# Turning the FFN's gated products with transposing transfers in place of TensorE transposes

## The chip, the cores and the metric

The kernel runs on one core of a Trainium2 chip. The core has five engines that work beside each other: TensorE (PE, matrix products; its weight loads are listed as PEld), VectorE (DVE), ScalarE (ACT), GpSimd (POOL) and SyncE (SP), which here issues transfers. Each engine takes its instructions in the order of its own queue, and they wait for each other on semaphores. Transfers between the device's memory and the on-chip memory SBUF run on 16 DMA engines. TensorE writes to PSUM, eight banks of 128 x 512 float32.

The metric is the device time of one execution in microseconds (us), as the median of several runs. Lower is better.

## The reference

The reference is an encoder trunk of two layers over 256 tokens of width 1024. Each layer has two mixing branches (gated linear attention and grouped-query attention), an output projection, a gated feed-forward block (FFN) and an embedding that is added per layer, each with RMS norms around it. What the change touches is the FFN, whose hidden width is 2816:

```python
gate, up = jnp.split(rms_norm(h, g_ffn_pre) @ w_ffn_in, 2, axis=-1)
h = h + rms_norm((jax.nn.silu(gate) * up) @ w_ffn_out, g_ffn_post)
```

## The kernel before

**Products in split form.** Every operand of a matmul is kept as two parts of TensorE's reduced float32 format: a high part, which is the value rounded, and a low part, which is what the rounding left. A product is three passes: high by high, high by low, low by high. `split` (line 133) makes the parts: ACT casts the value to the high part, DVE subtracts it from the value for the low part. Weights are loaded in units of 128 x 2048 float32 (1 MB) into `raw` tiles or lent buffers, split in two pieces of 128 x 1024, and held in four pairs of buffers `wh` and `wl`. `Stream` runs ahead: when a unit has been used, `ws.done()` lets the next unit be split (as long as fewer than four are held) and the next load be issued (line 296) on SP's queue.

**What is turned, and why.** A matmul contracts over the partition dimension. A result has tokens in partitions and columns of the hidden layer along the row; the next product needs the hidden columns in partitions. So the gated products, `silu(gate) * up`, are turned in blocks of 128 x 128. `transpose_in` (lines 440 to 449) does it: TensorE transposes against an identity matrix into one PSUM bank (`aux`), then ACT and DVE split the bank into the tile that holds the turned product in high and low parts (`Split.put`, line 133 again). These tiles belong to `hid`, a `Split`: group k // 4 holds four blocks of 128 hidden columns for both halves of the tokens.

**The FFN's order.** The 2816 hidden columns are 11 blocks of 256. Blocks 0 and 1 are computed first, one token half (128 tokens, `hf`) after the other (L1566 and the product behind it). Blocks 4, 5 and 10 (`PLAIN`) are computed by `block`, both halves together (L1584). The other six are three pairs, blocks 2 and 3, 6 and 7, 8 and 9 (`PAIRS`), computed by `seven`, a form of Strassen's method: seven products in place of eight, with sums of weights made on DVE and four sums of activations (`sums`) made once; `gated` (L1608) is called for one half at step 6 and for the other at step 7. The three strings of `FFN` set the order: `u` is half a plain block, a digit a step of a pair, `o` the product of one block with `w_ffn_out`, in the order of `OUT` = 0, 1, 2, 3, 4, 5, 10, 6, and then, in the stage `ffnout`, 7, 8, 9. `out_step` makes those output products (its matmuls are listed at L105, as those of the FFN's first product are at L121). It calls `hid.need`, which makes sure that the turned blocks it reads have been put into the program.

**Tasks and ticks.** A turn is a `Task`: a generator that yields how many ticks to wait. `tick()` is called twice in every 12 matmuls or so; at each tick the tasks whose count is over go on. Blocks 0 and 1 wait 4 ticks (`WAIT_FFN`), plain blocks 6 (`WAIT_BLOCK`, L1592 is their transpose), pairs 9 (`WAIT_PAIR`), the last pair 3 and 4 (`WAIT_LAST`).

**The planner.** The kernel's text gives the order in which instructions are written down, and from it their priority. A planner then orders each engine's queue: it simulates the engines and takes, among the instructions that it holds ready, the one of the highest priority. `tc.high_priority(AHEAD)` raises the priority of what stands under it; `tc.issue_after` fixes an order. The planner also puts in the waits and gives out the buffers: ten `mid` tiles (128 x 1024 float32), five `t512` tiles, nine `big` tiles, eight PSUM banks. An instruction that needs a buffer waits until one is free.

Of the kernel before, what the change touches and what calls it, by code (L numbers as in the profile page):

```python
# [10 lines left out]
F32 = mybir.dt.float32  # L11
F32R = mybir.dt.float32r
BF16 = mybir.dt.bfloat16
AF = mybir.ActivationFunctionType
ALU = mybir.AluOpType
AX = mybir.AxisListType

P = 128
T = 256
# [4 lines left out]

AHEAD, EMPTY, EMPTY_FIRST = 400, 100, 1600

WAIT, WAIT_FIRST, WAIT_FFN, WAIT_BLOCK = 6, 4, 4, 6

WAIT_NEXT, WAIT_IN, WAIT_H = (7, 9), ((6, 9), (6, 6)), ((3, 5), (3, 5))
WAIT_MIX = 3, 6  # L30
# [11 lines left out]
PLAIN, PAIRS = (4, 5, 10), (2, 6, 8)  # L42
OUT = (0, 1, 2, 3, 4, 5, 10, 6, 7, 8, 9)

WAIT_PAIR, WAIT_LAST = 9, (3, 4)


GATES = "uuu1u2m34m5m67m"
# [11 lines left out]
def trunk_kernel(ctx: ExitStack, tc: tile.TileContext, a: dict, out: bass.AP):  # L60
# [7 lines left out]
    nc = tc.nc  # L68
# [11 lines left out]
    part = ["start"]  # L80

    def nm(s):
        uid[0] += 1
        return f"{s}_{part[0]}_{uid[0]}"
# [4 lines left out]
    def mid(dt=F32):  # L89
        return b4p.tile([P, 1024], dt, tag="mid", name=nm("mid"))  # L90

    def acc():
        return accp.tile([P, 512], F32, tag="acc", name=nm("acc"))

    def aux():
        return accp.tile([P, 512], F32, tag="acc", name=nm("aux"))

    def t512():
        return smp.tile([P, 512], F32, tag="t512", name=nm("t512"), bufs=5)
# [25 lines left out]
    def vmul(out, in0, in1):  # L125
        nc.vector.tensor_tensor(out=out, in0=in0, in1=in1, op=ALU.mult)
# [4 lines left out]
    def split(hi, lo, src):  # L131

        return nc.scalar.copy(hi, src), nc.vector.tensor_tensor(out=lo, in0=src, in1=hi.bitcast(F32), op=ALU.subtract)  # L133


    h = cp.tile([P, 2, D], F32, tag="h", name="h")
    line = {}

    def on(e, f, *args, **kw):

        with tc.issue_after(line[e].ins) if e in line else nullcontext():
            line[e] = f(*args, **kw)

    seed = cp.tile([P, P], BF16, tag="seed", name="seed")
    on("pool", nc.gpsimd.memset, seed, 1.0)
    keep = cp.tile([P, 512], BF16, tag="keep", name="keep")
    on("dve", nc.vector.memset, keep, 1.0)
# [13 lines left out]
    ident = cp.tile([P, P], F32, tag="ident", name="ident")  # L161
# [279 lines left out]
    def transpose_in(sp, src, k, n, hf, plain=None):  # L441

        ps = aux()
        for i in range(n):
            nc.tensor.transpose(ps[:, i * P : (i + 1) * P], src[:, i * P : (i + 1) * P], ident)
        with tc.high_priority(AHEAD):
            sp.put(ps[:, : n * P], k, n, hf * P, P)
        if plain is not None:
            nc.scalar.copy(plain, ps[:, : n * P])

    last_pow = [None]

# [13 lines left out]
    def split_by(hi, lo, src, r):  # L466

        nc.scalar.activation(hi, src, AF.Copy, bias=0.0, scale=r)
        nc.vector.scalar_tensor_tensor(
# [5 lines left out]
    def row_rstd(parts, behind=None):  # L475
# [5 lines left out]
        for j, src in enumerate(parts):  # L481
# [9 lines left out]
            else:  # L491
                with tc.issue_after(behind.ins) if j and behind is not None else nullcontext():
                    last_square[0] = nc.scalar.activation(
                        junk[:, :n], src, AF.Square, scale=1.0 / 32.0, accum_out=ss[:, j : j + 1]
                    )
# [19 lines left out]
    def halves(t):  # L515
        return [t[:, j * 512 : (j + 1) * 512] for j in range(2)]
# [24 lines left out]
    def pre_gain(g, hf, sp, wait, to):  # L541
# [8 lines left out]
        with tc.high_priority(EMPTY):  # L550
            ss = small(2, "ss")
            for j in range(2):
                last_square[0] = nc.scalar.activation(t512(), x[j], AF.Square, scale=1.0 / 32.0, accum_out=ss[:, j : j + 1])
            r = rs[hf]
# [32 lines left out]
    def last_norm(parts, g, hf):  # L587

        with tc.high_priority(AHEAD):
            yt, junk, ss, r, c = mid(), mid(), small(3, "ss"), small(1, "rstd"), 0  # L590
            cuts = []
            for src in parts:
                cuts.append(slice(c, c + src.shape[-1]))
                c += src.shape[-1]
            nc.scalar.activation(junk[:, cuts[0]], parts[0], AF.Square, scale=1.0 / 32.0, accum_out=ss[:, 0:1])
            nc.vector.scalar_tensor_tensor(
# [16 lines left out]
            for j, c in enumerate(cuts):  # L613
                x = h[:, hf, c]
                if j == 1:
                    nc.scalar.activation(yt[j], yt[j], AF.Copy, bias=0.0, scale=r)
                    nc.gpsimd.tensor_tensor(out=x, in0=yt[j], in1=x, op=ALU.add)
# [4 lines left out]
    def amode(o, sp, hf, k0, w, first, last, c0=0, fresh=False):  # L622

        wh, wl = (t[:, :2048].rearrange("p (k c) -> p k c", c=512)[:, :, c0 : c0 + o.shape[-1]] for t in w)
        sp.need(hf, k0)
        parts = [(sp.tok(k0 + k, hf), (wh[:, k, :], wl[:, k, :])) for k in range(4)]
        passes(o, parts, first, last, fresh, tick if o.shape[-1] == 512 else None)
        tick()
# [100 lines left out]
    def project_t(sp):  # L729

        o = [acc(), acc()]
        for kh in range(2):
            wmode(o, sp, kh * 4, ws.take(), kh == 0, kh == 1)
            ws.done()
        return o

    def project(sp):

        o = [acc(), acc()]
        for kh in range(2):  # L740
            w = ws.take()
            for hf in range(2):
                amode(o[hf], sp, hf, kh * 4, w, kh == 0, kh == 1)
            ws.done()
        return o
# [97 lines left out]
    def square(hf, j):  # L843
        on("act", nc.scalar.activation, t512(), hv(hf, j), AF.Square, scale=1.0 / 32.0, accum_out=ss[hf][:, j : j + 1])

# [31 lines left out]
    def turn(hf, *ks):  # L877

        if (hf, ks[0] // 4) not in banks:
            banks[hf, ks[0] // 4] = aux()  # L880
        for k in ks:
            ps = banks[hf, k // 4][:, k % 4 * P : (k % 4 + 1) * P]
            on("pe", nc.tensor.transpose, ps, h[:, hf, k * P : (k + 1) * P], ident)
# [138 lines left out]
    for l in range(DEPTH):  # L1022
# [109 lines left out]
        o = {}  # L1132
# [139 lines left out]
        for x in range(2):  # L1272
            o = project_t(uT)
            for i in range(2):
                dst = qk[:, x, 2 * i : 2 * i + 2, :]
                src = o[i].rearrange("p (h t) -> p h t", t=T)
# [144 lines left out]
        for j in range(2):  # L1421
            o = project(uT)
# [124 lines left out]
        hid = Split()  # L1547
        us = [[ws.take() for _ in range(2)] for _ in range(2)]

        def turned(src, k, n, hf, wait=WAIT_FFN):  # L1550


            def turn():
                yield wait
                transpose_in(hid, src, k, n, hf)

            hid.makers[hf].append(Task(turn(), part[0], k // 4))

        for hf in range(2):
            ws.lend = hf == 1  # L1560
            for b in range(2):
                o = acc()
                for kh in range(2):
                    amode(o, u2, hf, kh * 4, us[b][kh], kh == 0, kh == 1, fresh=b == 0)
                sg = t512()
                nc.scalar.activation(sg[:, 0:256], o[:, 0:256], AF.Silu)  # L1566
                vmul(sg[:, 0:256], o[:, 256:512], sg[:, 0:256])
                turned(sg[:, 0:256], 2 * b, 2, hf)
                if hf == 1:
                    ws.done(2)  # L1570
                if (hf, b) == (1, 0):
                    forms = sums(plain)

        def block(b):
            sg = t512()
            o = [acc(), acc()]
            for kh in range(2):
                w = ws.take()
                for hf in range(2):
                    amode(o[hf], u2, hf, kh * 4, w, kh == 0, kh == 1)  # L1580
                if kh == 1:
                    for hf in range(2):
                        c = slice(hf * 256, (hf + 1) * 256)
                        nc.scalar.activation(sg[:, c], o[hf][:, 0:256], AF.Silu)  # L1584
                        vmul(sg[:, c], o[hf][:, 256:512], sg[:, c])

                    def turn():
                        yield WAIT_BLOCK
                        ps = aux()
                        for k in range(2):  # L1590
                            for hf in range(2):
                                nc.tensor.transpose(  # L1592
                                    ps[:, k * T + hf * P : k * T + (hf + 1) * P],
                                    sg[:, hf * 256 + k * P : hf * 256 + (k + 1) * P], ident,
                                )
                        with tc.high_priority(AHEAD):
                            hid.put(ps, 2 * b, 2, 0, T)

                    t = Task(turn(), part[0], 2 * b // 4)
                    for hf in range(2):  # L1600
                        hid.makers[hf].append(t)
                ws.done()
                yield

        def pair(b):
            def gated(hf, gate, up):
                sg = t512()
                nc.scalar.activation(sg, gate, AF.Silu)  # L1608
                vmul(sg, up, sg)
                turned(sg, 2 * b, 4, hf, WAIT_LAST[hf] if b == PAIRS[-1] else WAIT_PAIR)  # L1610

            return seven(u2, forms, gated)

        o = []
# [18 lines left out]

        outs = list(OUT)
        steps, pairs, seven_ = chain.from_iterable(block(b) for b in PLAIN), list(PAIRS), None
        for x in FFN:
            if x == "p":
                gpost = gain(a["g_ffn_post"][l], mid(), D)
                continue
            if x == "o":  # L1640
                n, w = outs.pop(0), ws.take()
# [117 lines left out]
```

## Time and profile before

| what | before |
|---|---|
| median of 3 runs | 917.91 us (917.15 to 918.28) |
| profiled execution, its own time | 916.88 us |
| its span, from the first to the last instruction | 914.8 us |
| granted TensorE clock, mean | 0.997 |
| FFN stage of the first layer | about 254 to 433 us of the span |
| FFN stage of the second layer | about 706 to 885 us of the span |

The prediction shows the lines. They are read so: a group of instructions has its line, engine and operation, then what it writes and reads by the program's names, the shapes, and how often; behind a bar its busy time and the mean in nanoseconds of one; behind a second bar the time that the engine was idle just before, and what ended most of it. In a list of waits the columns are who waited for whom, the total in us, how many times, and the longest. The chain that ended last is followed back from the last instruction; each piece has its start, its length, and what it was. A name ends in the stage (`_0ffnin`: layer 0, first FFN stage, and with it the output products 0 to 6). Durations of TensorE instructions overlap, since it works them in a pipeline.

### The profile page before, as it was taken

The numbers are of one execution on the slowest core, as the hardware profiler recorded it, in microseconds if no ns is written. First come the engines' busy times: TensorE is split into PE (matmuls) and PEld (weight loads), VectorE is DVE, ScalarE is ACT, GpSimd is POOL, SyncE is SP. The second block draws the span as 40 slices with busy tenths as digits, with TensorE's granted clock in tenths as the row PEclk, the third lists the DMA queues.
The fourth block names the chain that finished last, engine by engine and source line by source line (L and its number), as shares of the span: only waits on it lengthen the run. The fifth ranks groups of instructions, "written<-read, shape, count | busy, mean of one in ns | idle before, by whom it ended". The sixth has DMA issues, their size and how long they took to land.

```text
span 914.8 us, 12463 instructions
## 1 busy us (share of the span) xinstructions
PE 906.7 (99%) x4679; PEld 776.8 (85%) x4679; DVE 786.3 (86%) x1009; ACT 583.9 (64%) x971; POOL 99.9 (11%) x157
## 2 busy tenths in 40 slices
PE   9999999999999999999999999999999999999996
PEld 8998888888888888888899988888888888888886
DVE  7889989987679998999779789899876899989984
ACT  6688767465567565666676687675644766565563
POOL 3700220400100000000324001110001000000001
PEclk9999999999999999999999999999999999999998
DMA  8663445667385555657566424455573846555361
GB/s 285 213 201 121 139 140 189 214 186 255 123 297 182 197 191 205 228 169 262 176 249 231 138 92 139 138 184 184 196 253 123 277 164 215 219 172 222 134 234 47
DMA packets 89513, 173.47 MB, mean 190 GB/s; under 512 B 3486, under 2 KB 27558, under 8 KB 88940
## 3 DMA queue, kind: packets, MB, share of 16 engines
q1 hardware_dynamic: 89292, 172.53, 55.5%
q8 instruction: 37, 0.61, 0.3%
q14 instruction: 24, 0.20, 0.1%
q10 hardware_dynamic: 160, 0.14, 0.0%
HBM read 169.50 MB, written 3.15 MB: 189 GB/s over the span
## 4 chain that ended last, share of the span: by engine, by line
PE 95%; ACT 1%; DVE 1%; DMA 1%; issue 1%; POOL 0%; POOLq 0%
PE acc_1ffnin L121 12%; PE acc_0ffnin L121 12%; PE acc_1gate L121 7%; PE acc_0gate L121 7%; PE acc_1ffnin L105 7%; PE acc_0ffnin L105 7%; PE acc_0gqk L121 3%; PE acc_1gqk L121 3%; PE acc_0wout L121 2%; PE acc_1wout L121 2%; PE acc_1gg L121 2%; PE acc_0gg L121 2%; PE acc_1v L121 2%; PE acc_0v L121 2%; PE acc_1merge L121 2%; PE acc_0merge L121 2%
## 5 line engine op out<-in xcount | busy, mean ns | idle before, releaser
L133 ACT CAST wh_1ffnin<-raw_1ffnin 128x1024 fp32r<-128x1024 f32 x38 | 38.5, 1048 | 25.9 <-PE acc_1ffnin L105 10.2
L133 ACT CAST wh_0ffnin<-raw_0ffnin 128x1024 fp32r<-128x1024 f32 x38 | 38.2, 1048 | 25.1 <-PE acc_0ffnin L105 9.3
L133 DVE TENSOR_TENSOR wl_1ffnin<-raw_1ffnin,wh_1ffnin 128x1024 fp32r<-128x1024 f32 x38 | 45.0, 1221 | 7.6 <-ACT wh_1ffnin L133 7.4
L133 DVE TENSOR_TENSOR wl_0ffnin<-raw_0ffnin,wh_0ffnin 128x1024 fp32r<-128x1024 f32 x38 | 44.7, 1220 | 7.2 <-ACT wh_0ffnin L133 7.2
L105 PE MATMUL acc_1ffnin<-wh_1ffnin,big_1ffnin 128*128 128x512 f32 x176 | 45.1, 390 | 0.0
L105 PE MATMUL acc_0ffnin<-wh_0ffnin,big_0ffnin 128*128 128x512 f32 x176 | 45.1, 390 | 0.0
L121 PE MATMUL acc_1ffnin<-wh_1ffnin,big_1wout 128*128 128x512 f32 x168 | 42.5, 393 | 0.0
L121 PE MATMUL acc_0ffnin<-wh_0ffnin,big_0wout 128*128 128x512 f32 x168 | 42.5, 393 | 0.0
L105 PEld LDWEIGHTS acc_1ffnin<-wh_1ffnin,big_1ffnin 128*128 128x128 f32 x176 | 33.0, 188 | 6.9
L105 PEld LDWEIGHTS acc_0ffnin<-wh_0ffnin,big_0ffnin 128*128 128x128 f32 x176 | 33.0, 188 | 6.9
L133 DVE TENSOR_TENSOR wl_0ffnin<-lent_0ffnin,wh_0ffnin 128x1024 fp32r<-128x1024 f32 x30 | 35.8, 1218 | 2.2 <-ACT wh_0ffnin L133 2.2
L133 DVE TENSOR_TENSOR wl_1ffnin<-lent_1ffnin,wh_1ffnin 128x1024 fp32r<-128x1024 f32 x30 | 35.8, 1218 | 1.9 <-ACT wh_1ffnin L133 1.9
L121 PEld LDWEIGHTS acc_1ffnin<-wh_1ffnin,big_1wout 128*128 128x128 f32 x168 | 31.1, 188 | 6.2
L121 PEld LDWEIGHTS acc_0ffnin<-wh_0ffnin,big_0wout 128*128 128x128 f32 x168 | 31.1, 188 | 6.2
L133 ACT CAST wh_0ffnin<-lent_0ffnin 128x1024 fp32r<-128x1024 f32 x30 | 30.7, 1052 | 8.2 <-PE acc_0ffnin L105 3.9
L133 ACT CAST wh_1ffnin<-lent_1ffnin 128x1024 fp32r<-128x1024 f32 x30 | 30.7, 1052 | 7.5 <-PE acc_1ffnin L105 3.9
L133 ACT CAST wh_0gate<-raw_0gate 128x1024 fp32r<-128x1024 f32 x20 | 20.0, 1049 | 15.6 <-DMA raw_0gate<-in_w_o_attn_dram 6.5
L133 DVE TENSOR_TENSOR wl_0gate<-raw_0gate,wh_0gate 128x1024 fp32r<-128x1024 f32 x20 | 24.0, 1244 | 6.5 <-ACT wh_0gate L133 6.4
L133 ACT CAST wh_1gate<-raw_1gate 128x1024 fp32r<-128x1024 f32 x20 | 19.9, 1048 | 14.1 <-DMA raw_1gate<-in_w_o_attn_dram 6.3
L133 DVE TENSOR_TENSOR wl_1gate<-raw_1gate,wh_1gate 128x1024 fp32r<-128x1024 f32 x20 | 23.5, 1221 | 5.4 <-ACT wh_1gate L133 5.3
L105 PE MATMUL acc_0ffnin<-wl_0ffnin,big_0ffnin 128*128 128x512 f32 x88 | 24.6, 394 | 0.0
L105 PE MATMUL acc_1ffnin<-wl_1ffnin,big_1ffnin 128*128 128x512 f32 x88 | 24.6, 394 | 0.0
(724 smaller groups left out, 2711.3 us busy)
## 6 DMA issues: line engine op xcount, KB each, us to landing
raw_0ffnin<-in_w_ffn_out_dram SPq DMA_DIRECT2D x11, 1024.0 KB, 5.9
raw_1ffnin<-in_w_ffn_out_dram SPq DMA_DIRECT2D x11, 1024.0 KB, 5.4
lent_0ffnin<-in_w_ffn_in_dram SPq DMA_DIRECT2D x6, 1024.0 KB, 7.5
lent_1ffnin<-in_w_ffn_in_dram SPq DMA_DIRECT2D x6, 1024.0 KB, 7.8
raw_0v<-in_w_in_dram SPq DMA_DIRECT2D x4, 1024.0 KB, 5.1
raw_0gate<-in_w_o_gla_dram SPq DMA_DIRECT2D x4, 1024.0 KB, 5.9
raw_0gate<-in_w_o_attn_dram SPq DMA_DIRECT2D x4, 1024.0 KB, 5.2
raw_0wout<-in_w_ffn_in_dram SPq DMA_DIRECT2D x8, 512.0 KB, 4.7
```

The lines of the kernel that those rows point to most:

```text
L105: return nc.tensor.matmul(o, lhsT, rhs, start=start, stop=stop)
L121: nc.tensor.matmul(o, x, y, start=start and n == 0, stop=stop and n == len(seq) - 1, **kw)
L133: return nc.scalar.copy(hi, src), nc.vector.tensor_tensor(out=lo, in0=src, in1=hi.bitcast(F32), op=ALU.subtract)
```

## The change

In the FFN, all gated products but those of the last pair are turned in another way.

- `turn_out` takes a `mid` tile and cuts it in two halves. ACT copies the product's 512 columns, seen as 1,024 words of 16 bits, into the first half, so that all words of one significance stand together: two planes of 512. Then SP issues one transposing transfer of the 128 x 1,024 words, which turns the eight blocks of 128 x 128 words into the second half. Both stand under the raised priority.
- `take_in`, after 9 ticks (`WAIT_TURNED`), has ACT join the two planes to float32 again, into the first half, and splits that into `hid`, with the priority of its place.
- For a plain block (`hf` is None) the copy also puts the columns in the order of hidden block and token half, so that the turned tile has both halves of the tokens side by side.
- Blocks 0 and 1 now share one `t512` tile for each token half, and are turned together once block 1 is done.
- The last pair keeps `transpose_in`, with its waits of 3 and 4 ticks.
- `WAIT_FFN`, `WAIT_BLOCK` and `WAIT_PAIR` go.

```diff
+    def turn_out(src, k, hf):
+
+        with tc.high_priority(AHEAD):
+            both, turned = halves(mid())
+            turned = turned.bitcast(U16)
+            parts = both.bitcast(U16).rearrange("p (s c) -> p s c", s=2)
+            words = src.bitcast(U16)
+            if hf is None:
+                nc.scalar.copy(
+                    parts.rearrange("p s (k h f) -> p h k f s", k=2, f=P),
+                    words.rearrange("p (h k f s) -> p h k f s", h=2, f=P, s=2),
+                )
+            else:
+                nc.scalar.copy(parts.rearrange("p s c -> p c s"), words.rearrange("p (c s) -> p c s", s=2))
+            nc.sync.dma_start_transpose(out=turned.rearrange("p (x t) -> p x t", t=P), in_=parts.rearrange("p s c -> p (s c)"))
+        return both, turned
+
+    def take_in(sp, both, turned, k, hf):
+
+        n, tn = (2, T) if hf is None else (4, P)
+        hi, lo = sp.at(k, n, (hf or 0) * P, tn)
+        nc.scalar.copy(
+            both.bitcast(U16).rearrange("p (k t s) -> p k t s", s=2, t=tn),
+            turned.rearrange("p (s k t) -> p k t s", s=2, t=tn),
+        )
+        split(hi, lo, both.rearrange("p (k t) -> p k t", t=tn))
...
-        def turned(src, k, n, hf, wait=WAIT_FFN):
-
+        def turned(src, k, hf):
 
             def turn():
-                yield wait
-                transpose_in(hid, src, k, n, hf)
-
-            hid.makers[hf].append(Task(turn(), part[0], k // 4))
+                if k == 2 * PAIRS[-1]:
+                    yield WAIT_LAST[hf]
+                    transpose_in(hid, src, k, 4, hf)
+                else:
+                    x = turn_out(src, k, hf)
+                    yield WAIT_TURNED
+                    take_in(hid, *x, k, hf)
+
+            t = Task(turn(), part[0], k // 4)
+            for i in range(2) if hf is None else (hf,):
+                hid.makers[i].append(t)
...
+            first = t512()
             for b in range(2):
...
-                sg = t512()
-                nc.scalar.activation(sg[:, 0:256], o[:, 0:256], AF.Silu)
-                vmul(sg[:, 0:256], o[:, 256:512], sg[:, 0:256])
-                turned(sg[:, 0:256], 2 * b, 2, hf)
+                sg = first[:, b * 256 : (b + 1) * 256]
+                nc.scalar.activation(sg, o[:, 0:256], AF.Silu)
+                vmul(sg, o[:, 256:512], sg)
+                if b:
+                    turned(first, 0, hf)
...
-                    def turn():
-                        yield WAIT_BLOCK
-                        ps = aux()
-                        for k in range(2):
-                            for hf in range(2):
-                                nc.tensor.transpose(
-                                    ps[:, k * T + hf * P : k * T + (hf + 1) * P],
-                                    sg[:, hf * 256 + k * P : hf * 256 + (k + 1) * P], ident,
-                                )
-                        with tc.high_priority(AHEAD):
-                            hid.put(ps, 2 * b, 2, 0, T)
-
-                    t = Task(turn(), part[0], 2 * b // 4)
-                    for hf in range(2):
-                        hid.makers[hf].append(t)
+                    turned(sg, 2 * b, None)
...
-                turned(sg, 2 * b, 4, hf, WAIT_LAST[hf] if b == PAIRS[-1] else WAIT_PAIR)
+                turned(sg, 2 * b, hf)
```

More of the change, by code (lines that the diff above doesn't have):

```diff
@@ L13 @@
 BF16 = mybir.dt.bfloat16
+U16 = mybir.dt.uint16
 AF = mybir.ActivationFunctionType
@@ L25 @@
 AHEAD, EMPTY, EMPTY_FIRST = 400, 100, 1600
-WAIT, WAIT_FIRST, WAIT_FFN, WAIT_BLOCK = 6, 4, 4, 6
+WAIT, WAIT_FIRST = 6, 4
 WAIT_NEXT, WAIT_IN, WAIT_H = (7, 9), ((6, 9), (6, 6)), ((3, 5), (3, 5))
@@ L43 @@
 OUT = (0, 1, 2, 3, 4, 5, 10, 6, 7, 8, 9)
-WAIT_PAIR, WAIT_LAST = 9, (3, 4)
+WAIT_TURNED, WAIT_LAST = 9, (3, 4)
 GATES = "uuu1u2m34m5m67m"
```

## The prediction

> **What bounds the kernel now.** I read the page's busy times first, then the waits of PE, then the transposes by their tile, then the chain of work that ended last, and last the busy times by stretch.
>
> ```profile
> span 914.8 us, 12463 instructions
> PE 906.7 (99%) x4679; PEld 776.8 (85%) x4679; DVE 786.3 (86%) x1009; ACT 583.9 (64%) x971; POOL 99.9 (11%) x157
> ```
> ```profile
> PE warm L105 <- POOL seed L142: 1.0, 1, 1.0
> PE acc_1rq L121 <- DVE big_0ple L133: 0.2, 1, 0.2
> ```
>
> PE is busy for 99% of the span and waits 1.2 us in all, none of it in the FFN. So an instruction taken off PE in the FFN shortens the program by the time by which it holds up the next matmul, as long as what feeds PE keeps up. Two things feed it: the halves of the split weights (a cast on ACT, a subtraction on DVE) and the loads from the SP queue.
>
> ```profile
> L445 PE MATMUL aux_0ffnin<-ident,t_0ffnin x32: 270/271/273, 266.2 to 420.9; 128*128 128x128 f32 x32
> L133 DVE TENSOR_TENSOR big_0ffnin<-aux_0ffnin,big_0ffnin x13: 415/682/692, 269.8 to 421.8; 128x512 fp32r<-128x512 f32 x9, 128x256 fp32r<-128x256 f32 x4
> L1592 PE MATMUL aux_0ffnin<-ident,t_0ffnin x12: 270/272/273, 297.1 to 340.1; 128*128 128x128 f32 x12
> L445 PE MATMUL aux_1ffnin<-ident,t_1ffnin x32: 270/271/273, 718.1 to 872.8; 128*128 128x128 f32 x32
> L1592 PE MATMUL aux_1ffnin<-ident,t_1ffnin x12: 270/272/273, 749.1 to 792.1; 128*128 128x128 f32 x12
> ```
>
> These are the transposes of the gated products: 44 a layer. The last pair keeps its 8 (four for each token half), so 36 a layer, 72 in all, leave PE. Their 271 ns are not their price: matmuls overlap. The price stands in the chain, where the columns are start, length and piece.
>
> ```profile
> 283.39 0.22 PE aux_0ffnin L445 x2
> ...
> 297.23 0.44 PE aux_0ffnin L1592 x4
> ...
> 335.34 1.39 PE acc_0ffnin L105 x6
> 336.74 1.36 PE acc_0ffnin L121 x6
> 338.10 0.44 PE aux_0ffnin L445 x4
> 338.54 1.40 PE acc_0ffnin L121 x6
> ```
>
> A group of two holds PE for 0.22 us, a group of four for 0.44 us. Six matmuls directly behind a group take 1.39 to 1.40 us where six others take 1.36: about 0.03 us more per group.
>
> **The change, part by part.**
>
> PE, the gain. The groups that go are, in each layer, four of two (blocks 0 and 1, both halves), three of four (blocks 4, 5, 10) and four of four (the first two pairs, both halves): 4 x 0.22 + 7 x 0.44 = 3.96 us, and 11 x 0.03 = 0.33 us for the matmuls behind them. That is 4.29 us a layer and 8.6 us in both.
>
> ScalarE. Three rows price its work (mean ns is the number behind the comma):
>
> ```profile
> L133 ACT CAST wh_0ffnin<-raw_0ffnin 128x1024 fp32r<-128x1024 f32 x38 | 38.2, 1048 | 25.1 <-PE acc_0ffnin L105 9.3 <-PE acc_0ffnin L121 6.7 <-DMA raw_0ffnin<-in_w_ffn_out_dram 4.6
> L133 ACT CAST big_0ffnin<-aux_0ffnin 128x512 fp32r<-128x512 f32 x9 | 5.3, 585 | 10.0 <-PE aux_0ffnin L445 8.4 <-PE aux_0ffnin L1592 1.5
> L133 ACT CAST mid_0ffnin<-mid_0wout 128x512 fp32r<-128x512 f32 x3 | 1.7, 626 | 0.0
> L133 ACT CAST big_0ffnin<-aux_0ffnin 128x256 fp32r<-128x256 f32 x4 | 1.5, 369 | 0.0
> ```
>
> Blocks 0 and 1 now share a tile, so a layer has 9 turned tiles of 512 columns (2 + 3 + 4). Each gets a copy of 1,024 16-bit words that takes the planes apart and one that joins them. No row shows a copy of strided 16-bit words. The nearest is the 1,024-element cast, 1.048 us; half of it (paid by bytes) and twice it (the stride costs double) are the ends. I take 1.05 us, since 512 columns against 1,024 in these rows show that elements count: 18 x 1.05 = 18.9 us a layer. The high half is then cast from SBUF, 9 x 0.626 = 5.6 us, in place of 7 x 0.585 + 4 x 0.369 = 5.6 us from PSUM: nothing. So ACT gains 19 us a layer, 9 to 38 between the ends.
>
> DVE. The low halves go from 7 x 0.68 + 4 x 0.415 = 6.4 us to 9 x 0.68 = 6.1 us a layer. Nothing. The products themselves keep their shapes.
>
> ```profile
> 254.00:284.00 30.00, 30.00 (x142) 24.73 (x141) 23.50 (x32) 21.81 (x36) 0.86 (x2) 1.00 0.88 296
> 284.00:314.00 30.00, 30.00 (x136) 24.82 (x135) 28.88 (x27) 18.81 (x25) 0.00 (x0) 1.00 0.39 128
> 314.00:344.00 30.00, 30.00 (x142) 24.87 (x141) 27.74 (x29) 18.89 (x26) 0.95 (x1) 1.00 0.62 220
> 344.00:374.00 30.00, 30.00 (x134) 24.83 (x133) 26.33 (x24) 16.50 (x19) 0.00 (x0) 1.00 0.66 240
> 374.00:404.00 30.00, 30.00 (x138) 24.84 (x137) 27.77 (x24) 19.01 (x24) 0.00 (x0) 1.00 0.42 140
> 404.00:434.00 30.00, 30.00 (x141) 24.85 (x140) 28.28 (x32) 18.97 (x27) 0.87 (x2) 1.00 0.72 262
> ```
>
> The columns are span, then PE, PEld, DVE, ACT and POOL busy, clock, DMA share, GB/s. ACT has 114.0 us of work in these 180 us and gets 133, at the upper end 152: it has the room. DVE has 162.5 of 180 and is the engine with the least room behind PE, 17.5 us a layer. PE's 4.3 us come out of that and leave 13. What covers the added ACT work is therefore ACT's idle time; what could break is DVE, which goes hungry when ACT stands.
>
> The new waits. In its queue's order the joining copy waits for the transfer to land, and casts of weights stand behind it. Who waits for those is DVE, then PE.
>
> ```profile
> ACT wh_0ffnin L133 <- PE acc_0ffnin L105: 13.1, 5, 3.9
> DVE wl_0ffnin L133 <- ACT wh_0ffnin L133: 9.4, 11, 1.8
> SPq L296 <- DVE wl_0ffnin L133: 106.3, 21, 11.3
> ```
>
> ACT's own waits are mostly for PE to give a weight buffer back: the split weights are as far ahead as four buffers allow, so a stand of a few us finds stock.
>
> The transfers. SP gets 9 more issues a layer, each behind a wait for ACT's copy, with weight loads queued behind; SP itself mostly waits for DVE to free a buffer (106.3 us in the row above), so an issue as long as a plain one costs nothing.
>
> ```profile
> q1 hardware_dynamic: 20532, 41.93, 62.9%
> lent_0ffnin<-in_w_ffn_in_dram SPq DMA_DIRECT2D x6, 1024.0 KB, 7.5
> mid_0ffnout<-in_p_dram SPq DMA_DIRECT2D x1, 256.0 KB, 6.4
> L296 SPq DMA_DIRECT2D raw_0ffnin<-in_w_ffn_in_dram x11: 367/368/509, 276.1 to 374.2; - x11
> DMA to landing us min/median/max: 4.0/5.7/7.7
> ```
>
> No transposing transfer is in this trace. A tile is 128 x 1,024 x 2 bytes, 256 KB. The row of that size landed in 6.4 us; the shortest weight load, 512 KB or more, in 4.0 us. The other end is by packets: the queue's 20,532 packets in the 191 us from 254 to 445 took 62.9% of 16 engines, 94 ns each; in rows of 256 bytes a tile is 1,024 packets, 6.0 us of all 16 engines, and with the 6.4 us about 12 us. I take 6.4, the row of equal size. [...]
>
> Is PE ever late for the turned product? The tightest is the first pair's second half:
>
> ```profile
> 328.37 0.62 ACT L1608 ACTIVATE t_0ffnin<-mid_0ffnin 128x512 f32<-128x512 f32 x1
> ...
> 354.00 5.44 PE acc_0ffnin L105 x24
> ```
>
> Its product is done on DVE at about 329.7, and the output step that reads it (n = 2) starts at 354.0: 24 us for two copies, a transfer and a split, 1.05 + 6.4 + 1.05 + 0.63 + 0.68 = 9.8 us. With 12 us of landing it is 15.4. Nothing.
>
> Does the planner put the joining copy where the data has landed? It issues what it thinks ready ahead of its place in the program:
>
> ```profile
> 388.36 0.46 SPq L803 DMA_DIRECT2D mid_0ffnin<-in_w_alpha_up_dram  x1
> ...
> 402.70 1.05 ACT L805 CAST mid_0ffnin<-mid_0ffnin 81x1024 fp32r<-81x1024 f32 x1
> ...
> 409.34 5.44 PE acc_0ffnin L121 x24
> ```
>
> L803 and L805 stand in the program behind the last pair, whose last steps PE does from 409.34; they ran 21 and 7 us before. So the count of 9 ticks will not hold the joining copy back by itself; it sits where the planner expects the landing. In this row that was 14 us after the issue, without a stand. I take no loss, with the whole landing as the other end (first rival).
>
> Buffers. Each turned tile holds one of ten mid tiles for some 10 us. The sums of the pairs hold four, a pair's products two, the plain products two until the forms are made: with two turned tiles that is ten at the start of the FFN, so they just fit. PSUM banks come free. Nothing, unless the forms are held up.
>
> **The sum.** 8.6 us less. Against the profiled execution, 916.88 us (span 914.8 and 2.08 around it), that is 908.3; the median of the runs lies 1.03 above it, so 909.3. A few joins behind 1 MB loads (7.5 us) will show some hold; I leave 0.7 us for it: 910.0.
>
> **The rivals.**
>
> First, slower: ACT stands at the joining copy. If it stands h us each time, DVE finishes the two subtractions it has (2.4 us) and then goes hungry; a layer loses 9 (h - 2.4) - 17.5 us. With the gain counted it breaks even at h = 4.8 us. At the median landing, 5.7 us, it is 2 x 12.2 - 8.6 = 15.8 us slower: 934. For it: in-order ACT and a planner that may expect less. Against it: loads were met with little standing (4.6 us on the output weights in a layer).
>
> Second, slower: the transfers take the queue. At 6.0 us of all engines each they fill 54 of the 71 us (37.1% of 191) that the engines have free, and each weight load behind one comes 6.0 us late. By the same formula with h = 6.0 that is 2 x 14.9 - 8.6 = 21 us: 939. For it: the DMA share is 0.88 in the first stretch. Against it: 0.39 and 0.42 in two others. [...]
>
> Third, part of the gain: DVE, at 28.88 of 30 us in one stretch, cannot follow a faster PE everywhere. Half the gain: 913.6. Against it: it is idle 11 us between 284 and 434, where PE gains 3.3.
>
> Fourth, no change: the holds eat the gain, h near 4.8 us: 917.9.
>
> **Chances.** The forecast (908 to 912) 0.48; the third 0.09; the fourth 0.06; the first 0.19; the second 0.15; forms late for want of a mid tile 0.03, some 925. Faster 0.57, same 0.06, slower 0.37; 0.2% is 1.8 us, about what these runs can tell. The range goes from 908 to 938, which leaves out the longer holds of the first two rivals; the likeliest's own is 908 to 912.
>
> **What would show it.** Right: in both FFN stages no L1592 rows, L445 only for the last pair, the chain still PE throughout, PE without waits, ACT some 19 us a layer busier. Wrong: PE waiting for big_0ffnin or for wl; ACT standing over 4.8 us at each joining copy; issue-to-landing of the turned tiles over 10 us, or weight loads landing later than 7.7 us; an SP issue far above 0.37 us.

## The result and the profile after

| | before | after |
|---|---|---|
| median of the runs | 917.53 us (916.93 to 918.28) | 963.16 us (962.87 to 967.19) |
| ratio after to before | | 1.0507, 95% interval 1.0492 to 1.0522 |
| profiled execution | 916.88 us | 962.93 us |
| its span, mean granted clock | 914.8 us, 0.997 | 961.1 us, 0.982 |

The change makes the kernel 5% slower. 910.0 us was forecast, with a range from 908 to 938. Line numbers of the changed kernel lie one to some thirty higher: the first product is L122, the output L106, the split L134.

The first lines of the page after, and the waits of PE (who waited for whom, total us, times, longest):

```profile
span 961.1 us, 12377 instructions
PE 918.3 (96%) x4607; PEld 773.9 (81%) x4607; DVE 787.7 (82%) x1005; ACT 685.4 (71%) x1003; POOL 102.5 (11%) x157
```
```profile
PE acc_1ffnin L106 <- ACT wh_1ffnin L134: 7.1, 3, 4.8
PE acc_0ffnin L106 <- ACT wh_0ffnin L134: 6.5, 2, 4.1
PE acc_0ffnin L122 <- ACT wh_0ffnin L134: 6.4, 4, 3.7
PE acc_1ffnin L122 <- ACT wh_1ffnin L134: 5.9, 3, 3.6
PE acc_1ffnin L122 <- DVE wl_1ffnin L134: 4.2, 5, 1.4
PE acc_0ffnin L122 <- DVE wl_0ffnin L134: 3.8, 5, 1.4
PE warm L106 <- POOL seed L143: 1.0, 1, 1.0
PE acc_1ffnin L106 <- DVE wl_1ffnin L134: 0.8, 2, 0.4
```

PE's waits went from 1.2 to 35.7 us, all of the new ones in the FFN and all for split weights. PE's busy time went from 906.7 to 918.3. Together that is 34.5 + 11.6 = 46.1 us, the difference of the two profiled executions (46.05). The transposes did go from PE (4,607 instructions, 72 fewer), but those that stayed took longer: the first experiment below runs the same 4,607 instructions in 899.7 us, 18.6 us less. The busy times by stretch show why (columns: span, PE, PEld, DVE, ACT and POOL busy, clock, DMA share, GB/s):

```profile
284.00:314.00 30.00, 27.12 (x109) 21.01 (x108) 25.98 (x24) 28.04 (x26) 0.00 (x0) 0.94 0.49 144
314.00:344.00 30.00, 27.68 (x120) 21.99 (x120) 20.95 (x23) 24.28 (x20) 0.00 (x0) 1.00 0.56 184
344.00:374.00 30.00, 22.19 (x85) 16.77 (x84) 24.07 (x23) 27.90 (x26) 0.00 (x0) 0.83 0.52 161
```

Before, DVE had 26 to 29 of 30 us here and ACT 16 to 19. Now ACT has 24 to 28 of 30, and DVE goes hungry with 21 to 26. PE stands in all three stretches; in the first and the last its granted clock is lower too (0.94 and 0.83), so that a stand can cost more than its length. In the last stretch PE stands for 3.7 us until 351.8 and for 4.1 us until 358.9; the clock is 0.83, and four matmuls behind the second stand take 2.17 us where four take 1.07 us at 365.6. The longest stand, 4.8 us until 835.0 in the second layer, lies in a stretch with 0.83 as well (826 to 856), and four matmuls behind it take 2.17 us too. The first stretch has 0.94 although no stand there is longer than 1.4 us. How long a stand must be to lower the clock is not shown.

What filled ACT stands in its groups of 16-bit copies, and in the pieces of the chain that ended last:

```profile
L465 ACT COPY mid_0ffnin<-t_0ffnin 128x1024 uint16<-128x1024 uint16 x6 | 29.4, 4892 | 0.4 <-DVE t_0ffnin L127 0.3
L460 ACT COPY mid_0ffnin<-t_0ffnin 128x1024 uint16<-128x1024 uint16 x3 | 14.5, 4842 | 0.0
L473 ACT COPY mid_0ffnin<-mid_0ffnin 128x1024 uint16<-128x1024 uint16 x9 | 10.6, 1177 | 6.0 <-DMA mid_0ffnin<-mid_0ffnin 6.0
```
```profile
267.50 4.89 ACT mid_0ffnin L465
272.41 3.28 DMA mid_0ffnin<-mid_0ffnin
...
284.63 4.91 ACT mid_0ffnin L465
289.56 3.08 DMA mid_0ffnin<-mid_0ffnin
```

The copy that takes the planes apart (L465 and L460) takes 4.88 us, the one that joins them (L473) 1.18 us, with the same number of words of the same type. The apart copy goes through the product in order and writes one word to the one plane, the next to the other, 1,024 bytes away. The joining copy reads by turns and writes in order. The transfer between them is short:

```profile
L466 SPq DMA_TRANSPOSE mid_0ffnin<-mid_0ffnin x9: 1232/1238/1354, 272.4 to 404.4; - x9
...
DMA to landing us min/median/max: 3.1/3.1/3.1
```

### The profile page after: what moved, and what is told of

It reads as the page before. It is cut to its first block, busy times and chain, and to the rows that moved or that the text cites. A ratio compares the mean times of both kernels' runs of the same rounds, so it can differ in the third digit from the quotient of the medians.

```text
span 961.1 us, 12377 instructions
## 1 busy us (share of the span) xinstructions
PE 918.3 (96%) x4607; PEld 773.9 (81%) x4607; DVE 787.7 (82%) x1005; ACT 685.4 (71%) x1003; POOL 102.5 (11%) x157
## 4 chain that ended last, share of the span: by engine, by line
PE 69%; ACT 10%; DVE 9%; issue 6%; DMA 6%; POOL 0%; POOLq 0%; SPq 0%; ACTq 0%; DVEq 0%
PE acc_1gate L122 7%; PE acc_0gate L122 7%; PE acc_1ffnin L122 5%; PE acc_1ffnin L106 4%; DVE wl_0ffnin L134 3%; ACT wh_0ffnin L134 3%; PE acc_1rq L122 2%; PE acc_0gqk L122 2%; PE acc_1gqk L122 2%; PE acc_0ffnin L106 2%; PE acc_0wout L122 2%; PE acc_1wout L122 2%; PE acc_0ple L122 2%; PE acc_1gg L122 2%; PE acc_0gg L122 2%
## 5 line engine op out<-in xcount | busy, mean ns | idle before, releaser
L106 PE MATMUL acc_1ffnin<-wh_1ffnin,big_1ffnin 128*128 128x512 f32 x176 | 47.7, 406 | 7.1 <-ACT wh_1ffnin L134 7.1
L106 PE MATMUL acc_0ffnin<-wh_0ffnin,big_0ffnin 128*128 128x512 f32 x176 | 47.6, 406 | 6.5 <-ACT wh_0ffnin L134 6.5
L134 ACT CAST wh_1ffnin<-raw_1ffnin 128x1024 fp32r<-128x1024 f32 x38 | 38.1, 1047 | 19.6 <-DVE mid_1ffnin L721 5.4
L134 ACT CAST wh_0ffnin<-raw_0ffnin 128x1024 fp32r<-128x1024 f32 x38 | 37.9, 1047 | 19.8 <-DMA raw_0ffnin<-in_w_ffn_out_dram 6.6
L134 DVE TENSOR_TENSOR wl_1ffnin<-raw_1ffnin,wh_1ffnin 128x1024 fp32r<-128x1024 f32 x38 | 44.8, 1219 | 7.5 <-ACT wh_1ffnin L134 7.5
L134 DVE TENSOR_TENSOR wl_0ffnin<-raw_0ffnin,wh_0ffnin 128x1024 fp32r<-128x1024 f32 x38 | 44.6, 1219 | 5.3 <-ACT wh_0ffnin L134 5.0
L106 PEld LDWEIGHTS acc_1ffnin<-wh_1ffnin,big_1ffnin 128*128 128x128 f32 x176 | 34.0, 196 | 16.1 <-ACT wh_1ffnin L134 9.1
L106 PEld LDWEIGHTS acc_0ffnin<-wh_0ffnin,big_0ffnin 128*128 128x128 f32 x176 | 33.9, 196 | 15.4 <-ACT wh_0ffnin L134 8.6
L122 PE MATMUL acc_0ffnin<-wh_0ffnin,big_0wout 128*128 128x512 f32 x168 | 43.4, 402 | 2.1 <-ACT wh_0ffnin L134 2.1
L122 PE MATMUL acc_1ffnin<-wh_1ffnin,big_1wout 128*128 128x512 f32 x168 | 43.1, 400 | 1.4 <-ACT wh_1ffnin L134 1.4
L134 DVE TENSOR_TENSOR wl_0ffnin<-lent_0ffnin,wh_0ffnin 128x1024 fp32r<-128x1024 f32 x30 | 35.8, 1217 | 8.6 <-ACT wh_0ffnin L134 8.5
L122 PEld LDWEIGHTS acc_0ffnin<-wh_0ffnin,big_0wout 128*128 128x128 f32 x168 | 32.1, 193 | 10.1 <-ACT wh_0ffnin L134 3.4
L134 DVE TENSOR_TENSOR wl_1ffnin<-lent_1ffnin,wh_1ffnin 128x1024 fp32r<-128x1024 f32 x30 | 35.8, 1217 | 5.3 <-ACT wh_1ffnin L134 5.2
L122 PEld LDWEIGHTS acc_1ffnin<-wh_1ffnin,big_1wout 128*128 128x128 f32 x168 | 32.5, 195 | 8.9 <-ACT wh_1ffnin L134 2.0
L134 ACT CAST wh_1ffnin<-lent_1ffnin 128x1024 fp32r<-128x1024 f32 x30 | 30.8, 1060 | 5.3 <-DMA lent_1ffnin<-in_w_ffn_in_dram 2.6
L134 ACT CAST wh_0ffnin<-lent_0ffnin 128x1024 fp32r<-128x1024 f32 x30 | 30.9, 1073 | 3.0 <-DVE lent_0ffnin L332 2.6
L134 ACT CAST wh_0gate<-raw_0gate 128x1024 fp32r<-128x1024 f32 x20 | 19.9, 1048 | 14.9 <-DMA raw_0gate<-in_w_o_attn_dram 6.2
L465 ACT COPY mid_1ffnin<-t_1ffnin 128x1024 uint16<-128x1024 uint16 x6 | 29.3, 4881 | 0.8 <-DVE t_1ffnin L127 0.8
L465 ACT COPY mid_0ffnin<-t_0ffnin 128x1024 uint16<-128x1024 uint16 x6 | 29.4, 4892 | 0.4 <-DVE t_0ffnin L127 0.3
L134 ACT CAST wh_1gate<-raw_1gate 128x1024 fp32r<-128x1024 f32 x20 | 19.9, 1048 | 13.6 <-DMA raw_1gate<-in_w_o_attn_dram 5.7
L122 PE MATMUL acc_1ffnin<-wh_1ffnin,mid_1ffnin 128*128 128x512 f32 x96 | 24.8, 399 | 4.5 <-ACT wh_1ffnin L134 4.5
L134 DVE TENSOR_TENSOR wl_0gate<-raw_0gate,wh_0gate 128x1024 fp32r<-128x1024 f32 x20 | 24.0, 1246 | 5.7 <-ACT wh_0gate L134 5.6
```

The source lines that it names most:

```text
L106: return nc.tensor.matmul(o, lhsT, rhs, start=start, stop=stop)
L122: nc.tensor.matmul(o, x, y, start=start and n == 0, stop=stop and n == len(seq) - 1, **kw)
L465: nc.scalar.copy(parts.rearrange("p s c -> p c s"), words.rearrange("p (c s) -> p c s", s=2))
```

## The experiments

The first theory was that the apart copy's 4.88 us on ACT are the whole loss, and that its order of writing makes them. The rivals were those of the prediction: ACT standing at the joins until the transfers land, and the transfers taking the queue from the weight loads. All ratios below are against the kernel before on the same chip. Behind the first experiment, where a text says "plane by plane" or "plane order", the lines of the kernel are shown against that experiment, otherwise against the changed kernel; "..." stands for lines left out.

**Plane by plane.** The apart copy goes through one plane after the other, so that it writes in order and reads every second word.

```diff
-                    parts.rearrange("p s (k h f) -> p h k f s", k=2, f=P),
-                    words.rearrange("p (h k f s) -> p h k f s", h=2, f=P, s=2),
+                    parts.rearrange("p s (k h f) -> p s k h f", k=2, f=P),
+                    words.rearrange("p (h k f s) -> p s k h f", h=2, f=P, s=2),
...
-                nc.scalar.copy(parts.rearrange("p s c -> p c s"), words.rearrange("p (c s) -> p c s", s=2))
+                nc.scalar.copy(parts, words.rearrange("p (c s) -> p s c", s=2))
```

> One change to the changed kernel: the copy that takes the planes apart runs plane by plane, so that it writes its 1,024 words one behind the other and reads every second one; before, it read in order and wrote the two planes by turns. First theory (the time is ScalarE's, spent in writing by turns): the copy falls from 4.88 us to about 1.2 us, as in the joining copy, which already reads by turns and writes in order at 1.17 us; PE's waits in the FFN go, and the kernel lands at 908 to 916 us, below the kernel before. Rival (ScalarE stands at the joins until the transfers have landed, or the transfers hold up the weight loads): waits and time stay, 940 us or more, even if the copy is shorter. Third possibility (16-bit words at a stride are slow on either side): the copy stays near 4.9 us and the time near 963.

Measured: 911.66 us, ratio 0.9945 (0.9926 to 0.9964), clock 0.998.

```profile
span 909.2 us, 12377 instructions
PE 899.7 (99%) x4607; PEld 768.9 (85%) x4607; DVE 784.6 (86%) x1005; ACT 619.7 (68%) x1003; POOL 107.8 (12%) x157
```
```profile
L473 ACT COPY mid_0ffnin<-mid_0ffnin 128x1024 uint16<-128x1024 uint16 x9 | 10.5, 1170 | 9.7 <-DMA mid_0ffnin<-mid_0ffnin 9.7
L465 ACT COPY mid_0ffnin<-t_0ffnin 128x1024 uint16<-128x1024 uint16 x6 | 6.3, 1046 | 0.5 <-DVE t_0ffnin L127 0.4
L460 ACT COPY mid_0ffnin<-t_0ffnin 128x1024 uint16<-128x1024 uint16 x3 | 3.1, 1042 | 0.0
```

The copy is down to 1.04 us, PE waits 1.2 us in the FFN (three times 0.4 us, for DVE), and the kernel is faster than before, by 0.6%. The order of one loop was worth 51.5 us. ACT stands longer at the joins here (9.7 against 6.0 us in this layer) while the time falls, so that rival is out.

**The apart copy beside PE's transposes.** The transposes stay on PE; the copy is made as in the changed kernel, and nothing uses it.

```diff
-            nc.sync.dma_start_transpose(out=turned.rearrange("p (x t) -> p x t", t=P), in_=parts.rearrange("p s c -> p (s c)"))
...
-                    x = turn_out(src, k, hf)
-                    yield WAIT_TURNED
-                    take_in(hid, *x, k, hf)
+                    turn_out(src, k, hf)
+                    if hf is not None:
+                        yield 9 if k else 4
+                        transpose_in(hid, src, k, 4, hf)
+                        return
+                    yield 6
+                    ps = aux()
...
+                    with tc.high_priority(AHEAD):
+                        hid.put(ps, k, 2, 0, T)
```

> The transposes stay on PE, as before the change (blocks 0 and 1 in one group of four), and the copy that takes the planes apart, in its slow order, is made beside them; its result is not used. No transfers, no joins. First theory: 18 copies of 4.88 us on ScalarE cost nearly all that the change cost, less the joins: 940 to 965 us. Rival (joins and transfers): 918 to 925 us.

Measured: 961.95 us, ratio 1.0481 (1.0466 to 1.0497), with no transfer and no join in the program. The row of copies, and the two longest waits of PE:

```profile
L465 ACT COPY mid_0ffnin<-t_0ffnin 128x1024 uint16<-128x1024 uint16 x6 | 29.3, 4877 | 2.6 <-DVE t_0ffnin L127 2.6
```
```profile
PE acc_1ffnin L122 <- DVE big_1ffnin L134: 5.6, 1, 5.6
PE acc_0ffnin L122 <- DVE big_0ffnin L134: 5.2, 1, 5.2
```

The apart copies by themselves cost 44.3 us. That the time is within 1.2 us of the changed kernel's is in part luck: here PE still does its transposes, ACT makes no joins, and PE's longest waits are not for weights but for DVE's split of a turned tile, in the first layer behind an apart copy that held ACT from 351.2 to 355.9 us.

**The transfers beside PE's transposes.** As in the last experiment, with the transfer and without the copy.

```diff
+            nc.sync.dma_start_transpose(out=turned.rearrange("p (x t) -> p x t", t=P), in_=src.bitcast(U16))
```

> The transposes stay on PE, and the 18 transposing transfers are issued beside them, straight from the product's bytes; their result is not used, and there is no copy and no join. First theory: 1.24 us of SP and about 3 us of the queue each are covered: 917 to 921 us. Rival (the transfers hold up the weight loads): 930 us or more.

Measured: 916.96 us, ratio 0.9993 (0.9983 to 1.0002): no cost of the transfers shows.

```profile
q1 hardware_dynamic: 108300, 177.25, 58.2%
```
```profile
DMA to landing us min/median/max: 3.7/4.3/5.6
```

The queue worked off 19,008 more packets than before, 1,056 for each transfer. Its share of the 16 engines' span went from 55.5% of 914.8 to 58.2% of 915.3 us: 25 us in all, 1.4 us a transfer. The second rival is out.

**How the loss goes with the number of slow copies.** Plane by plane, but for the three plain blocks of a layer.

```diff
-                    parts.rearrange("p s (k h f) -> p s k h f", k=2, f=P),
-                    words.rearrange("p (h k f s) -> p s k h f", h=2, f=P, s=2),
+                    parts.rearrange("p s (k h f) -> p h k f s", k=2, f=P),
+                    words.rearrange("p (h k f s) -> p h k f s", h=2, f=P, s=2),
```

> Plane by plane, but in the three plain blocks of a layer, where the copy writes by turns as in the changed kernel: 6 slow copies in place of 18. If the loss goes with the number of copies (51.5 us for 18), 911.7 + 17.2 = 929 us. If there is a cover that must be used up first (by the formula of the prediction's first rival, 3 x (3.8 - 2.4) = 4.2 us a layer against 17.5 us of DVE idle time), 911 to 914 us. PE's clock stays at 0.997 in the second case.

Measured: 928.56 us, ratio 1.0119 (1.0105 to 1.0134). Against the plane order six slow copies cost 16.9 us, 2.8 each (by the ratios 16.0); eighteen cost 51.5, 2.9 each. Between these two counts the loss goes with the number of copies, and no cover shows that is used up first.

**Is it the place of the copy?** The changed kernel without the raised priority around the copy and the transfer.

```diff
-        with tc.high_priority(AHEAD):
-            both, turned = halves(mid())
+        both, turned = halves(mid())
```

> The changed kernel with its slow copy, but the copy and the transfer have the priority of their place, not the raised one. If the 4.88 us hurt because they are put ahead of the weight casts, and ScalarE has idle time for them elsewhere (as the prediction reckoned: room for up to 38 us a layer), the time falls well below 963, to 920 to 940 us. If ScalarE has no such room, it stays at 955 to 965 us.

Measured: 960.56 us, ratio 1.0476 (1.0463 to 1.0490). ACT is as full as with the raised priority:

```profile
284.00:314.00 30.00, 27.14 (x109) 21.03 (x108) 26.05 (x26) 28.98 (x27) 0.00 (x0) 0.94 0.48 149
344.00:374.00 30.00, 22.58 (x79) 17.34 (x78) 23.94 (x23) 26.83 (x24) 0.00 (x0) 0.83 0.40 126
```

The same was done to the plane order.

> The same for the plane order. If the raised priority of a copy of 1.05 us costs casts that DVE waits for, 909 to 911 us; if not, 911 to 913 us.

Measured: 914.43 us (911.85 to 920.13), ratio 0.9975 (0.9962 to 0.9988). That is above both times that were expected. Its own place is no better there; the raised priority is not what holds the plane order back.

**What makes writing by turns slow.** Three kernels, all of them with the plane order elsewhere. In the first the joining copy reads each plane in order and writes every second word, 4 bytes on.

```diff
-            both.bitcast(U16).rearrange("p (k t s) -> p k t s", s=2, t=tn),
-            turned.rearrange("p (s k t) -> p k t s", s=2, t=tn),
+            both.bitcast(U16).rearrange("p (c s) -> p s c", s=2),
+            turned.rearrange("p (s c) -> p s c", s=2),
```

> The copy that takes apart runs plane by plane (so it writes in order); the copy that joins, which read by turns and wrote in order at 1.17 us, now reads each plane in order and writes every second word. If writing 16-bit words that do not stand side by side is what is slow, whatever the distance, the joining copy goes from 1.17 to some 4.8 us and the kernel back to 950 to 965 us. If it is only the turning between two places 1,024 bytes apart with each word, the copy stays at 1.2 us and the kernel at 911 to 912 us.

In the others the apart copy goes through a plane in steps of eight words, 16 bytes, and of four words, 8 bytes (shown with eight).

```diff
-                nc.scalar.copy(parts, words.rearrange("p (c s) -> p s c", s=2))
+                nc.scalar.copy(parts.rearrange("p s (q r) -> p s r q", r=8), words.rearrange("p (q r s) -> p s r q", r=8, s=2))
```

> Plane by plane, but in the tiles of the pairs and of blocks 0 and 1 the copy that takes apart goes through a plane in steps of eight words, so that each write lands 16 bytes behind the last, in one plane. [...] If it is only the turning between two far places, all take 1.05 us and the time stays at 911 to 912 us.

> The same in steps of four words: each write 8 bytes behind the last, two of them in the same 16 bytes. [...] If every write that does not follow on the last is slow, they take as long as with 16 bytes.

Measured: 911.49 us for the joining copy by planes, ratio 0.9934 (0.9921 to 0.9947); 943.79 us with 16 bytes and 919.93 with 8 (one execution each). With 16 bytes in one plane the copy is as slow as by turns between two places 1,024 bytes apart (4.88 us both), and with 8 bytes it takes about half as long (2.55 against 4.88 us), so not every write that does not follow on the last is equally slow. The copies concerned, in that order:

```profile
L473 ACT COPY mid_0ffnin<-mid_0ffnin 128x1024 uint16<-128x1024 uint16 x9 | 12.3, 1364 | 10.2 <-DMA mid_0ffnin<-mid_0ffnin 10.2
```
```profile
L465 ACT COPY mid_0ffnin<-t_0ffnin 128x1024 uint16<-128x1024 uint16 x6 | 29.3, 4876 | 0.4 <-DVE t_0ffnin L127 0.3
```
```profile
L465 ACT COPY mid_0ffnin<-t_0ffnin 128x1024 uint16<-128x1024 uint16 x6 | 15.3, 2554 | 0.4 <-DVE t_0ffnin L127 0.3
```

| successive writes in the same 16 bytes | copy of 1,024 words | per 16 bytes begun |
|---|---|---|
| one (by turns 1,024 bytes apart; or 16 bytes on) | 4.88 us; 4.88 us | 4.8 ns |
| two (8 bytes on) | 2.55 us | 5.0 ns |
| four (4 bytes on) | 1.36 us | 5.3 ns |
| eight (in order) | 1.04 us | |

It is not a distance beyond 16 bytes and not the type: each change to another 16 bytes on the writing side costs ACT about 5 ns in these copies (4.8 to 5.3 in the table). Reading by turns costs next to nothing (1.17 against 1.04 us). In the two copies with steps the reads step as well, 32 and 16 bytes on; that this adds nothing was not tried by itself. It can't cost what a write does: with 8 bytes each read is in another 16 bytes too, and the copy takes half of 4.88 us.

**The copy on GpSimd.** Plane by plane, with `nc.gpsimd.tensor_copy` in both branches of `turn_out` (one is shown).

```diff
-                nc.scalar.copy(parts, words.rearrange("p (c s) -> p s c", s=2))
+                nc.gpsimd.tensor_copy(parts, words.rearrange("p (c s) -> p s c", s=2))
```

> Plane by plane, and the copy that takes apart is made on GpSimd, busy for 12% of the span, in place of ScalarE. If what keeps the plane order at 911.7 and not at the 909.3 of the sum is ScalarE's added 19 us a layer, 909 to 911 us; if it is the landing and the joins, 911 to 913 us; if GpSimd needs over 5 us a copy or gets in DVE's way at the memory, slower than 913 us.

Measured: 930.45 us, ratio 1.0142 (1.0117 to 1.0167). The mean in the group below, 3.7 us a copy, comes from one copy of 12.1 us (at 285.45); the other eight of this layer take 1.6 to 3.0 us. ACT's joins stand 31.1 us for transfers, 11.6 of them behind that one copy:

```profile
L465 POOL COPY mid_0ffnin<-t_0ffnin 128x1024 uint16<-128x1024 uint16 x6 | 22.5, 3747 | 79.2 <-DVE t_0ffnin L127 67.4 <-issue 11.8
L473 ACT COPY mid_0ffnin<-mid_0ffnin 128x1024 uint16<-128x1024 uint16 x9 | 10.5, 1169 | 31.1 <-DMA mid_0ffnin<-mid_0ffnin 31.1
```

Here the stands at the joins, the prediction's first rival, do show; the planner put the joins ahead of where the data landed. The copy of 12.1 us lay beside work of DVE without a gap, from 284.97 to 296.67, and ended 0.9 us behind it; that DVE held it up is read from these times, not tried. How much of the 18.8 us over the plane order is theirs and how much is DVE's added work (795.7 against 784.6 us) stays open.

**The last pair too.** Plane by plane.

```diff
-                if k == 2 * PAIRS[-1]:
-                    yield WAIT_LAST[hf]
-                    transpose_in(hid, src, k, 4, hf)
-                else:
-                    x = turn_out(src, k, hf)
-                    yield WAIT_TURNED
-                    take_in(hid, *x, k, hf)
+                x = turn_out(src, k, hf)
+                yield WAIT_LAST[hf] if k == 2 * PAIRS[-1] else WAIT_TURNED
+                take_in(hid, *x, k, hf)
```

> Plane by plane, and the last pair is turned by transfers as well, with its waits of 3 and 4 ticks. PE loses 8 more transposes a layer, 0.94 us, 1.9 us in all. The way from the product to the turned tile is 1.05 + 3.1 to 6 (landing) + 1.17 + 0.62 + 0.68 us, 7 to 10 us, against about 7 us until the output step that reads the first half: if PE waits for it, 912 to 918 us; if it does not, 910 us.

Measured: 928.74 us, ratio 1.0120 (1.0105 to 1.0135), more than the worst that was expected. PE waits 2.5 and 2.7 us for the turned tile (`big`), and then, behind the output, for the norm (`h`), 6.8 us in the first layer:

```profile
PE aux_0ffnout L446 <- DVE h L608: 6.8, 1, 6.8
PE acc_1ffnin L106 <- ACT big_1ffnin L134: 2.7, 1, 2.7
PE acc_0ffnin L106 <- ACT big_0ffnin L134: 2.5, 1, 2.5
```

**The low halves on GpSimd.** Plane by plane.

```diff
-        split(hi, lo, both.rearrange("p (k t) -> p k t", t=tn))
+        src = both.rearrange("p (k t) -> p k t", t=tn)
+        nc.scalar.copy(hi, src)
+        nc.gpsimd.tensor_tensor(out=lo, in0=src, in1=hi.bitcast(F32), op=ALU.subtract)
```

> Plane by plane, and the low halves of the turned products (9 a layer, 0.68 us each on DVE) are subtracted on GpSimd, which can read them now that they stand in SBUF. If what keeps the plane order 2.4 us from the sum is DVE, which is busy for 29.1 of 30 us in two stretches, 909 to 911 us. If GpSimd's work slows DVE (18 copies on GpSimd raised DVE's busy time from 785 to 796 us), 911 to 914 us.

Measured: 920.84 us, ratio 1.0051 (1.0035 to 1.0067), above both times that were expected. DVE's subtraction of 128 x 1,024 went from 1.22 to 1.35 us on the mean in this group, so DVE's busy time rose (790.0 against 784.6 us) although 18 subtractions were taken from it:

```profile
L479 POOL TENSOR_TENSOR big_0ffnin<-mid_0ffnin,big_0ffnin 128x512 fp32r<-128x512 f32 x9 | 27.1, 3024 | 108.3 <-ACT big_0ffnin L478 108.3
...
L134 DVE TENSOR_TENSOR wl_0ffnin<-raw_0ffnin,wh_0ffnin 128x1024 fp32r<-128x1024 f32 x38 | 49.8, 1353 | 7.2 <-ACT wh_0ffnin L134 7.1
```

It is the subtractions beside GpSimd's that grew. The one at 343.94 us took 2.29 us and ended 1.1 us after GpSimd's, which ran from 342.09 to 345.15; those at 332.63 and 334.37, with GpSimd idle, took 1.21.

## Why the prediction was wrong, point by point

**The failed step** is the price of the apart copy: "The nearest is the 1,024-element cast, 1.048 us; half of it (paid by bytes) and twice it (the stride costs double) are the ends." The copy took 4.88 us, outside both ends. The rows that were taken are of casts that write in order. That price does hold for the plane order (1.04 us) and roughly for the joins (1.18 us). A stride was costed as one thing, reading and writing alike, and the order in which the loop walks the output was not looked at. The runs set the two sides apart: one write in each 16 bytes took 4.88 us, two 2.55 us, still 2.4 times the copy in order, while reading by turns took 1.17 us.

**A second step** would have hidden the error: "What covers the added ACT work is therefore ACT's idle time", with 152 of 180 us at the upper end. ACT's idle time was no such cover. With the price as measured the formula of the first rival still gives no loss: each copy 3.84 us longer, 9 x (3.84 - 2.4) = 13.0 us a layer against DVE's 17.5. The loss was 51.5 us, and three slow copies a layer, 11.5 us more on ACT, already cost 2.8 us each. A copy of 4.88 us keeps the next casts from DVE, and DVE, with 26 to 29 of 30 us of work, can't make that up; then PE stands, up to 4.8 us for a high half, and its clock falls (0.83 over the 30 us around that stand). So "a stand of a few us finds stock" did not hold either. Neither the raised priority nor the copy's own place changes that.

**What held.** PE's side, for the most part: in the plane order PE waits for hardly anything and its busy time is 7.0 us shorter than before (899.7 against 906.7), where the sum had 8.6. No run takes the transposes off PE alone, so the price of 8.6 us itself is not shown. SP's issue takes 1.24 us instead of 0.37, and nothing came of it (ratio 0.9993 with the transfers alone). The landing was 3.1 to 5.6 us in the changed kernel, the plane order and the run with the transfers alone, where 6.4 was taken and 12 was the other end. There are 1,056 packets a tile, near the 1,024 of the upper bound, but they take 1.4 us of the engines instead of 6.0. The 24 us until the turned product is read were enough.

**The rivals.** The first (stands at the joins) came to 6.0 us in one layer and 2.1 in the other, over 18 joins, far from 4.8 us each. The second (the queue) is refuted by the transfers alone, 916.96 us. The third (DVE can't follow) is what the plane order points to: it gains 5.85 us in the profiled executions, not 8.6. Forms late for want of a `mid` tile do not show there either: PE's few waits are not for them. Between 284 and 344 us the kernel before, and then the plane order:

```profile
284.00:344.00 60.00, 60.00 (x276) 49.69 (x275) 56.62 (x55) 37.70 (x50) 0.95 (x1) 1.00 0.51 174
```
```profile
284.00:344.00 60.00, 59.10 (x258) 47.66 (x257) 58.16 (x57) 48.78 (x62) 0.00 (x0) 1.00 0.67 202
```

Twenty of the 276 were transposes, so PE did 256 matmuls there before and 258 now, where the 2.2 us of transposes had room for some ten. DVE is at 58.2 of 60 us, and the 1.2 us for which PE waits in the FFN are for its low halves. That DVE is the bound in this stretch is read from these rows; the attempt to unload it onto GpSimd slowed DVE and so can't confirm it.

## What to carry to other kernels

Price a strided copy on ACT by where successive writes land, not by its element count: choose the loop order that writes in order and let the reads stride (1.04 against 4.88 us here). An engine with a third of its time idle (ACT, busy for 64% before) is still no cover for a long instruction (4.88 us) when it hands work to an engine that is 90% busy (DVE, 162.5 of 180 us before). Where a kernel is bound by one engine, work taken off it pays only as far as the next engine can follow; here that is the likely reading of 5.85 us gained where 8.6 were reckoned, not a shown one.

## What the runs showed of the hardware

- ACT's copy of 1,024 16-bit words in SBUF took 4.88, 2.55, 1.36 and 1.04 us with one, two, four and eight successive writes in the same 16 bytes. In the first three that is 4.8 to 5.3 ns for each change to another 16 bytes. Reading by turns and writing in order took 1.17 us.
- A transposing transfer of 128 x 1,024 words of 16 bits in SBUF took 1.24 us of SP and 1.4 us of the 16 engines and landed after 3.1 to 5.6 us. Eighteen of them beside the weight loads cost the kernel no time (916.96 us, ratio 0.9993).
- Transposes on PE of 271 ns each stand in the chain before with only 0.11 us (a group of two 0.22 us, a group of four 0.44 us).
- DVE's subtractions of 128 x 1,024 took longer with GpSimd's subtractions in the program: 1.22 us on the mean before, 1.35 in one layer and 1.28 in the other with them, and 2.29 us for one that began beside one of them. A copy on GpSimd that lay beside unbroken work of DVE took 12.1 us, the other eight of that layer 1.6 to 3.0.
